# Issuing the branch projections' 512-column matmuls as two of 256 columns into halves of one bank

## The chip, the cores and the metric

The kernel runs on one core of a Trainium2 chip. The metric is the device time of one execution in microseconds (us). Of the kernel before, three runs gave 668.11, 668.73 and 669.14 us, so the median is 668.73 us. The profile is one further execution of the same program, whose span from the first to the last instruction is 666.6 us.

## The reference, cut to what matters

The kernel computes one decoder layer with two parallel branches, in float32, for 256 tokens and a model width of 2048. An attention branch and a gated-MLP branch each give a 256x1024 matrix; each is gated by a SiLU and multiplied by its own projection matrix, and the two results are merged under sigmoid gates:

```python
y_a = (att * jax.nn.silu(z_a)) @ w_proj_a          # (256, 1024) @ (1024, 2048)
y_b = (sgu * jax.nn.silu(z_b)) @ w_proj_b          # (256, 1024) @ (1024, 2048)
merged = jax.nn.sigmoid(g_a) * y_a + jax.nn.sigmoid(g_b) * y_b
return x + merged @ w_out
```

The change touches the two products with `w_proj_a` and `w_proj_b` alone; the big input projection `h @ w_in` and the output product with `w_out` stay as they are.

## The kernel before, in words

**The number format.** Every float32 weight tile and every activation is split into a high part, rounded to the format float32r, and a low part, the remainder (`wh` and `wl`; `zah`, `zal`, `zbh`, `zbl`). ACT makes the high part with a copy and DVE the low part with a subtraction (lines 125 and 126). A product is then three float32r matmuls, low x high, high x high and high x low, into the same accumulator. That is the helper `three` (line 302), whose single `nc.tensor.matmul` at line 307 issues nearly all matmuls of the kernel, so that the profile shows them all under L307 and the tile names tell them apart.

**The stages.** `schedule()` lists 120 weight tiles of 128x2048 in the order in which they are used: the projections q, k, v, za, vb, ub and zb, then four rounds, c = 0 to 3, of a gate projection ("g", eight tiles) and a branch projection ("proj", four tiles), and at the end the output product ("out", sixteen tiles). Most "quad" tiles go through a Strassen-like scheme (`seven`, accumulators named `seven_...` and `acc_...`) or the plain scheme (`direct`).

**The branch projections.** In round c, the tiles q = 0 and 1 belong to `w_proj_a` and q = 2 and 3 to `w_proj_b`; each gives 512 output columns of four 128-row blocks of the contraction. `mm_rows` (line 542) walks over the four blocks `kk` and the two halves `m` of the tokens and calls `three` for each: 4 x 2 x 3 = 24 matmuls a tile, 96 a round, 384 in all. A matmul has a stationary 128x128 piece of `zah`, `zal`, `zbh` or `zbl` (loaded into the array by the matmul itself; the profile shows the load as an own row, LDWEIGHTS on PEld), and 512 moving columns of `wh` or `wl`. It accumulates into a PSUM bank of 512 float32, the tile `y`; a round has four of them, in four of the eight banks.

**Around them.** `turn_z` transposes the gated branch outputs on TensorE (`ps_zb`, line 412) and splits them into high and low parts (lines 506 and 507); for the second branch it runs in the first round's projection, through two banks in turn. After a round's last projection tile `merge` (line 532) multiplies the four banks by the gates and adds them, on DVE. `turn_m` (`ps_mT`) transposes the merged result for the output product.

**What sets the order.** The program is written in the order of the tiles, with side work hung on at given tiles by `at(...)`. Loads of weight tiles are issued on SP three tiles ahead, splits on ACT and DVE two tiles ahead. From the ninth tile on, the order within each engine's queue is decided by the tile framework's scheduler; each engine then works through its own queue in that order, and semaphores hold an instruction back until its inputs and its buffer are ready.

Of the kernel before, what the change touches and what calls it, by code (L numbers as in the profile page):

```python
# [29 lines left out]
B = 512  # L30
# [37 lines left out]
def hybrid_layer_kernel(  # L68
# [9 lines left out]
    nc = tc.nc  # L78
# [24 lines left out]
    raw, wh, wl, th, tl = {}, {}, {}, {}, {}  # L103
# [198 lines left out]
    def three(acc, hi, lo, bh, bl, start, stop, first=False):  # L302
        order = ((lo, bh), (hi, bh), (hi, bl))
        if first:
            order = ((hi, bh), (lo, bh), (hi, bl))
        for n, (a, b) in enumerate(order):
            nc.tensor.matmul(acc, a, b, start=(start and n == 0), stop=(stop and n == 2))  # L307

    BLK = {"12": 0, "11": 1, "22": 2, "21": 3}

    def direct(L, hs, ls, i, kp, start, stop):
# [5 lines left out]
        for c, kh in order:  # L317
            r, col = c // 2, c % 2
            hi = hs[t][:, a + kh, r * P:(r + 1) * P]
            lo = ls[t][:, a + kh, r * P:(r + 1) * P]  # L320
            o = BLK[f"{kh + 1}{col + 1}"] * B
            three(L[c], hi, lo, wh[i][:, o:o + B], wl[i][:, o:o + B], start[c == 3] and kh == 0, stop and kh == 1,
                  first=(i == 0))

    def seven(E, L, i, kp, first, last, started, hs, ls, Fh, Fl):
# [11 lines left out]
        def W(b):  # L337
            o = (BLK[b] - 1) * B
            return wh[i][:, o:o + B], wl[i][:, o:o + B]
# [202 lines left out]
    def mm_rows(acc, hl, i, kts, k0, first, last, by_row=False):  # L542

        order = [(kk, m) for kk in range(4) for m in range(2)]
        if by_row:
            order = [(kk, m) for m in range(2) for kk in range(4)]
        for kk, m in order:
            hi, lo = hl(k0 + kk, m)
            three(acc[m], hi, lo, wh[i][:, kk * B:(kk + 1) * B], wl[i][:, kk * B:(kk + 1) * B],
                  first and kk == 0, last and kk == 3)  # L550

    xres = {}

# [17 lines left out]
    first = {}  # L571
# [91 lines left out]
    for i, (kind, name, c, kp, n) in enumerate(G):  # L663
# [8 lines left out]
        if kind == "quad":  # L672
# [10 lines left out]
            if strassen(i):  # L683
                last = 4 if name == "g" else SK[-1]
# [20 lines left out]
        elif kind == "proj":  # L705
            if n % 2 == 0:
                Y = (Y if n else []) + [bank(E[n + m], f"y{n}_{c}{m}") for m in range(2)]
            z = ("za", "zb")[n // 2]

            def hl(k, m):  # L710
                return (X[z + "h"][:, k, m * P:(m + 1) * P], X[z + "l"][:, k, m * P:(m + 1) * P])

            mm_rows(Y[n // 2 * 2:], hl, i, None, 4 * (n % 2), n % 2 == 0, n % 2 == 1)
            if n == 3:
                merge(c, Y)
        for fn, a in later.pop(i, []):
            a = list(a)
# [66 lines left out]
```

## Time and profile before

| | us |
|---|---|
| median of three runs | 668.73 |
| span of the profiled execution | 666.6 |
| PE busy (matmuls) | 653.9 |
| PEld busy (weight loads) | 539.5 |
| DVE busy | 613.9 |
| ACT busy | 427.1 |

The profile has a page and views that are asked for. On the page, the busy time of an engine is the union of its instructions. The chain of waits goes back from the last instruction, at each step to whatever released it; its pieces have a start, a length, and what they were. A group row gives line, engine, operation, out<-in, the shapes and the count, then the busy time and the mean duration of one. Matmuls are pipelined and their ends are modelled: a matmul row of 512 columns lasts 389 ns though the next one starts 227 ns after it, so that the pace of a stretch is read from starts or from chain pieces (length over count), not from durations.

### The profile page before, as it was taken

To read this page: it belongs to the slowest core of one execution; us is meant where nothing else is said; L and a number is where in the kernel's file an instruction comes from. 1 tells how busy PE (TensorE), PEld (TensorE's weight loads), DVE (VectorE), ACT (ScalarE), POOL (GpSimd) and SP (SyncE) were. 2 spreads that over 40 slices of the span, in tenths; PEclk is the share of its full clock that TensorE was granted. 3 is DMA by queue.
4 is the path that set the end of the run, shared out by engine and by line. 5 is a ranking of instruction groups with operands and counts; after the bars stand their busy time and mean duration, and the time that the engine had idled before them with its cause. 6 is when DMAs were issued, how large, how long until landed. Compare 5 with 4: busy or idle time off the path is not lost.

```text
span 666.6 us, 7860 instructions
## 1 busy us (share of the span) xinstructions
PE 653.9 (98%) x2982; PEld 539.5 (81%) x2982; DVE 613.9 (92%) x606; ACT 427.1 (64%) x563; POOL 30.6 (5%) x28
## 2 busy tenths in 40 slices
PE   8799999999999999999999999999999999999997
PEld 4678888888888888888888788888888888888886
DVE  4589999999999699999999999979989989998996
ACT  7778968856895579774656835555564556746460
POOL 1000501300001004000000000000000000000000
PEclk9989999999999999999999999999999999999999
DMA  8962574555455624744546544935583574747641
GB/s 312 418 228 89 220 255 173 198 196 190 166 182 190 252 69 184 276 165 183 197 145 277 210 132 184 329 116 189 190 331 115 191 270 162 252 148 290 200 183 63
DMA packets 22213, 135.32 MB, mean 203 GB/s; under 512 B 2464, under 2 KB 3104, under 8 KB 7072
## 3 DMA queue, kind: packets, MB, share of 16 engines
q1 hardware_dynamic: 21024, 132.73, 54.1%
q10 hardware_dynamic: 1152, 2.10, 1.0%
q8 instruction: 23, 0.38, 0.2%
q14 instruction: 14, 0.11, 0.0%
HBM read 132.72 MB, written 2.10 MB: 202 GB/s over the span
## 4 chain that ended last, share of the span: by engine, by line
PE 75%; DVE 13%; DMA 5%; issue 4%; ACT 2%; SPq 0%; POOL 0%; DVEq 0%; ACTq 0%
PE acc_g L307 12%; PE y L307 11%; PE acc_out L307 9%; PE seven_g L307 6%; PE acc_v L307 4%; PE acc_k L307 4%; PE acc_za L307 4%; PE acc_ub L307 4%; PE acc_q L307 4%; PE seven_out L307 3%; DMA raw<-in_w 3%; DVE tl L157 3%; PE acc_vb L307 3%; DVE wl L126 2%; DMA xnat<-in_x 2%
## 5 line engine op out<-in xcount | busy, mean ns | idle before, releaser
L154 ACT CAST th<-t 128x1024 fp32r<-128x1024 f32 x104 | 109.3, 1054 | 114.1 <-DVE t L143 57.3
L126 DVE TENSOR_TENSOR wl<-raw,wh 128x2048 fp32r<-128x2048 f32 (+2 forms) x76 | 156.1, 2061 | 21.9 <-ACT wh L125 21.7
L125 ACT CAST wh<-raw 128x2048 fp32r<-128x2048 f32 (+2 forms) x76 | 130.8, 1729 | 47.9 <-PE acc_g L307 18.4
L157 DVE TENSOR_TENSOR tl<-t,th 128x1024 fp32r<-128x1024 f32 x104 | 126.2, 1217 | 3.3 <-ACT th L154 3.3
L155 DVE TENSOR_TENSOR wlp<-raw,whp 128x1536 fp32r<-128x1536 f32 x52 | 91.0, 1750 | 7.1 <-ACT whp L152 7.1
L152 ACT CAST whp<-raw 128x1536 fp32r<-128x1536 f32 x52 | 76.8, 1480 | 29.8 <-DMA raw<-in_w 15.1
L143 DVE TENSOR_TENSOR t<-raw 128x1024 f32<-128x1024 f32 x52 | 63.2, 1216 | 0.2
L307 PE MATMUL acc_g<-wl,xh 128*128 128x512 f32 x96 | 37.4, 389 | 0.0
L307 PE MATMUL acc_g<-wh,xh 128*128 128x512 f32 x96 | 37.4, 389 | 0.0
L307 PE MATMUL acc_g<-wh,xl 128*128 128x512 f32 x96 | 37.3, 389 | 0.0
L146 DVE TENSOR_TENSOR t<-t,raw 128x512 f32<-128x512 f32 x52 | 35.8, 689 | 0.3
L145 DVE TENSOR_TENSOR t<-t,raw 128x512 f32<-128x512 f32 x52 | 35.8, 689 | 0.2
L243 POOL TENSOR_TENSOR rs<-ms,mhalf 128x4 f32<-128x4 f32 x12 | 22.4, 1884 | 122.0 <-DVE ms L242 122.0
L307 PE MATMUL acc_q<-wh,xuh 128*128 128x512 f32 x64 | 25.9, 405 | 0.9 <-ACT wh L125 0.9
L307 PE MATMUL acc_q<-wl,xuh 128*128 128x512 f32 x64 | 26.0, 407 | 0.4 <-DVE wl L126 0.4
L307 PE MATMUL y<-wh,zbl 128*128 128x512 f32 x64 | 25.2, 394 | 0.8 <-DVE zbl L507 0.8
L307 PE MATMUL acc_q<-wh,xul 128*128 128x512 f32 x64 | 25.7, 401 | 0.0
L307 PE MATMUL y<-wh,zal 128*128 128x512 f32 x64 | 25.1, 392 | 0.0
L307 PE MATMUL y<-wl,zah 128*128 128x512 f32 x64 | 25.0, 391 | 0.0
L307 PE MATMUL y<-wl,zbh 128*128 128x512 f32 x64 | 24.9, 390 | 0.0
L307 PE MATMUL y<-wh,zbh 128*128 128x512 f32 x64 | 24.9, 390 | 0.0
L307 PE MATMUL acc_out<-wh,mh 128*128 128x512 f32 x64 | 24.9, 389 | 0.0
(502 smaller groups left out, 1598.4 us busy)
## 6 DMA issues: line engine op xcount, KB each, us to landing
raw<-in_w SPq DMA_DIRECT2D x116, 1024.0 KB, 4.8
raw<-in_w SPq DMA_DIRECT2D x7, 512.0 KB, 8.7
xnat<-in_x SPq DMA_DIRECT2D x2, 1024.0 KB, 13.5
xres<-in_x ACTq DMA_DIRECT2D x8, 256.0 KB, 4.7
out<-out_c SPq DMA_DIRECT2D x5, 256.0 KB, 2.5
xt<-in_xT SPq DMA_DIRECT2D x2, 512.0 KB, 8.5
xt<-in_xT SPq DMA_DIRECT2D x3, 256.0 KB, 9.0
raw<-in_w SPq DMA_DIRECT2D x2, 256.0 KB, 4.2
```

Source lines behind the costliest of these rows:

```text
L125: nc.scalar.copy(h, r)
L126: nc.vector.tensor_tensor(l, r, f(h), op=ALU.subtract)
L143: nc.vector.tensor_tensor(two, r[:, B:3 * B].rearrange("p (a n) -> p a n", a=2), r[:, None, 0:B].to_broadcast([P, 2, B]), op=ALU.add)
L145: nc.vector.tensor_tensor(t[:, 2 * B:3 * B], t[:, 0:B], r[:, 2 * B:3 * B], op=ALU.add)
L146: nc.vector.tensor_tensor(t[:, 3 * B:], t[:, 2 * B:3 * B], r[:, 3 * B:], op=ALU.add)
L152: nc.scalar.copy(wh[i], r[:, B:])
L154: nc.scalar.copy(th[i][:, sl], t[:, sl])
L155: nc.vector.tensor_tensor(wl[i], r[:, B:], f(wh[i]), op=ALU.subtract)
L157: nc.vector.tensor_tensor(tl[i][:, sl], t[:, sl], f(th[i][:, sl]), op=ALU.subtract)
L243: nc.gpsimd.tensor_tensor(dst, ms[:, :n], mhalf[:, :n], op=ALU.pow)
L307: nc.tensor.matmul(acc, a, b, start=(start and n == 0), stop=(stop and n == 2))
```

## The change

`mm_rows` calls a new helper, `three_halves`, in place of `three`. It issues the same three products in the same order, each as two matmuls of 256 moving columns, the first into columns 0 to 255 of the bank and the second into columns 256 to 511. Both have the same stationary piece. Only the first of the six matmuls that open a bank carries the start flag; the group check of the framework is switched off for these matmuls.

```diff
+    def three_halves(acc, hi, lo, bh, bl, start, stop):
+        for n, (a, b) in enumerate(((lo, bh), (hi, bh), (hi, bl))):
+            for h in range(2):
+                sl = slice(h * (B // 2), (h + 1) * (B // 2))
+                nc.tensor.matmul(acc[:, sl], a, b[:, sl], start=(start and n == 0 and h == 0),
+                                 stop=(stop and n == 2), skip_group_check=True)
+
...
         for kk, m in order:
             hi, lo = hl(k0 + kk, m)
-            three(acc[m], hi, lo, wh[i][:, kk * B:(kk + 1) * B], wl[i][:, kk * B:(kk + 1) * B],
-                  first and kk == 0, last and kk == 3)
+            three_halves(acc[m], hi, lo, wh[i][:, kk * B:(kk + 1) * B], wl[i][:, kk * B:(kk + 1) * B],
+                         first and kk == 0, last and kk == 3)
```

The 384 matmul instructions become 768. The framework's scheduler also puts some of the work around them in another order. Three places show it. The first is TensorE's queue in the first round's projection, where `turn_z` transposes the second branch (`ps_zb`, four transposes a row) between projection matmuls (`y`). Before:

```order
L307 MATMUL y_00_3007<-wh_2965,zah 128x512
L307 MATMUL y_00_3007<-wl_2966,zah 128x512
L307 MATMUL y_01_3008<-wh_2965,zal 128x512
L307 MATMUL y_01_3008<-wh_2965,zah 128x512
L412 MATMUL ps_zb_3049<-ident,zb_c_2653 128x128 x4
L307 MATMUL y_01_3008<-wl_2966,zah 128x512
L412 MATMUL ps_zb_3056<-ident,zb_c_2652 128x128 x4
L307 MATMUL y_00_3007<-wh_2965,zal 128x512
```

And of the change, at the same place (a row that ends in x2 is the two halves):

```order
L313 MATMUL y_00_3007<-wh_2965,zal 128x256 x2
L313 MATMUL y_00_3007<-wh_2965,zah 128x256 x2
L313 MATMUL y_00_3007<-wl_2966,zah 128x256
L419 MATMUL ps_zb_3073<-ident,zb_c_2653 128x128 x4
L313 MATMUL y_00_3007<-wl_2966,zah 128x256
L313 MATMUL y_01_3008<-wh_2965,zal 128x256
L419 MATMUL ps_zb_3080<-ident,zb_c_2652 128x128 x4
L313 MATMUL y_01_3008<-wh_2965,zal 128x256
L313 MATMUL y_01_3008<-wh_2965,zah 128x256 x2
```

The third group of transposes stands two and a half old matmuls earlier, the fourth still one old matmul behind it, so eight and a half old matmuls (as halves) are now left behind the fourth where there were six.

The second place is DVE's queue near the end of the gate projection of round 2. `tl` is the low part of the last Strassen tile of that projection, `wl` the low part of a plain tile that is needed later. Before:

```order
L155 TENSOR_TENSOR wlp_3760<-raw_3713,whp_3759 128x1536
L126 TENSOR_TENSOR wl_3793<-raw_3753,wh_3792 128x2048
L157 TENSOR_TENSOR tl_3762<-t_3755,th_3761 128x1024
L126 TENSOR_TENSOR wl_3820<-raw_3790,wh_3819 128x2048
L354 TENSOR_TENSOR g_h<-seven_g_1_3652,g_c_3844 128x512
```

And of the change, for the same tiles under other buffer numbers:

```order
L155 TENSOR_TENSOR wlp_3952<-raw_3905,whp_3951 128x1536
L157 TENSOR_TENSOR tl_3954<-t_3947,th_3953 128x1024
L126 TENSOR_TENSOR wl_3985<-raw_3945,wh_3984 128x2048
L126 TENSOR_TENSOR wl_4012<-raw_3982,wh_4011 128x2048
L361 TENSOR_TENSOR g_h<-seven_g_1_3844,g_c_4036 128x512
```

The second half of `tl` is now ahead of both plain tiles, one 128x2048 subtraction earlier.

The third place is TensorE's queue at the start of the output product, just behind the last projection matmul. `seven_out` and `acc_out` are its accumulators. Before:

```order
L307 MATMUL seven_out_0_4538<-wlp_4423,mh_4383 128x512
L307 MATMUL acc_out_2_4537<-th_4424,ml_4384 128x512
L307 MATMUL acc_out_2_4537<-th_4424,mh_4383 128x512
L307 MATMUL acc_out_0_4535<-whp_4422,ml_4384 128x512
L307 MATMUL acc_out_0_4535<-whp_4422,mh_4383 128x512
```

And of the change:

```order
L307 MATMUL seven_out_0_4922<-wlp_4759,mh_4719 128x512
L307 MATMUL acc_out_0_4919<-whp_4758,ml_4720 128x512
L307 MATMUL acc_out_0_4919<-whp_4758,mh_4719 128x512
L307 MATMUL acc_out_0_4919<-wlp_4759,mh_4719 128x512
L307 MATMUL acc_out_1_4920<-whp_4758,Flm 128x512
```

The two matmuls into `acc_out_2` have moved some nine matmuls back; the group of matmuls at the start of this stage is otherwise the same work.

## The prediction, as it was made before the run

> **What bounds the kernel now.** I read the page's busy shares first, then the chain of waits, then the projection's own rows.
>
> ```profile
> PE 653.9 (98%) x2982; PEld 539.5 (81%) x2982; DVE 613.9 (92%) x606; ACT 427.1 (64%) x563; POOL 30.6 (5%) x28
> ...
> PEclk9989999999999999999999999999999999999999
> ```
>
> TensorE is busy for 98% of the span and DVE for 92%, so the shares alone do not say which of the two decides in the rounds that the change touches. There are as many weight loads as matmuls (2982 each): every matmul brings its own load. The granted clock is at the upper level, 2.4 GHz, all along but for one early slice. The chain, in order of time (start, length, what), settles the first question:
>
> ```profile
> 378.63 0.80 issue
> 379.43 0.69 DVE zbl L507
> 380.17 11.21 PE y L307 x48
> ...
> 431.50 21.76 PE y L307 x96
> ...
> 493.38 21.76 PE y L307 x96
> ...
> 555.26 10.88 PE y L307 x48
> 566.15 1.75 PE ps_mT L412 x16
> 567.89 5.50 PE y L307 x24
> ...
> 574.26 5.46 PE y L307 x24
> ...
> 651.04 11.57 PE acc_out L307 x51
> ```
>
> From 380.17 us to the end of the matmuls every piece is TensorE's own. In the pieces shown stand 48 + 96 + 96 + 48 + 24 + 24 = 336 of the 384 projection matmuls (`y`). Whatever these cost more or less goes straight to the end. The other 48, the first branch of round 0, lie ahead of 379.43, where the chain hangs on DVE. The **pace** of a projection matmul is 21.76 / 96 = 226.7 ns.
>
> ```profile
> 431.34 0.39 PE L307 MATMUL y<-wh,zal 128*128 128x512 f32 x1
> 431.34 0.19 PEld L307 LDWEIGHTS y<-wh,zah 128*128 128x128 f32 x1
> ...
> 431.57 0.39 PE L307 MATMUL y<-wh,zah 128*128 128x512 f32 x1
> 431.57 0.19 PEld L307 LDWEIGHTS y<-wl,zah 128*128 128x128 f32 x1
> ```
>
> These timeline rows show how the two units interleave: the load for the next matmul (`zah`) begins when the present one (`zal`) begins, lasts 0.19 us, and is over some 40 ns before the next matmul starts. So 512 columns hide their load, and the stream of columns sets the pace. With 256 columns the stream is half as long and the load is not.
>
> **What the change does to this.** It removes 384 matmuls of 512 columns and adds 768 of 256, with 768 loads in place of 384. The bytes, the sums and the banks are the same. The question is one number, the pace of a 256-column matmul with its load; 113.3 ns would make no difference. No row of before has this shape, so I bound it. What the load alone allows is shown by the attention scores, 128 columns of plain f32, each record with a load of its own:
>
> ```profile
> 154.40 5.36 PE ps_s L435 x48
> ...
> L435 PEld LDWEIGHTS ps_s<-kT,qT 128*128 128x128 f32 x48 | 5.5, 192 | 0.1
> L307 PEld LDWEIGHTS y<-wh,zah 128*128 128x128 f32 x64 | 12.0, 188 | 2.4
> ```
>
> The scores run at 5.36 / 48 = 111.7 ns a record, though their load rows last 192 ns against the projection's 188: most of a load's row is latency, and one load every 111.7 ns can be had. The transposes (`ps_mT`, 1.75 / 16 = 109.4 ns, quoted above) come to nearly the same.
>
> The **lower bound** is then 111.7 ns: a pair takes 223.3, 3.3 ns less than one matmul before, and 336 x 3.3 = 1.1 us is gained.
>
> For the **upper bound** I ask what in 226.7 ns belongs to the columns and what to the instruction. The early slice at the lower clock helps:
>
> ```profile
> 36.44 0.63 PE L307 MATMUL acc_q<-wh,xuh 128*128 128x512 f32 x1
> ...
> 36.87 0.63 PE L307 MATMUL acc_q<-wl,xuh 128*128 128x512 f32 x1
> ...
> 37.30 0.63 PE L307 MATMUL acc_q<-wh,xul 128*128 128x512 f32 x1
> ```
>
> At 1.2 GHz the same form is issued every 0.43 us, which is 512 columns at one column a cycle (426.7) and nothing else. At 2.4 GHz that would be 213.3; the row says 226.7, so 13.4 ns are extra at the upper level. If all of this were a fixed cost of an instruction, a half would take 106.7 + 13.4 = 120.1 ns, a pair 240.1, and 336 x 13.4 = 4.5 us would be lost. If all of it went with the columns (operand data that cannot be read as fast as the array takes it), a half would take 113.3 and nothing would change. The short records decide where I stand: if a transpose of 128 columns is 256 cycles of array time (106.7 ns), only 109.4 - 106.7 = 2.7 ns of its pace are the instruction's. They also carry four bytes an element, and pay no 13 ns. I **take 2.7 ns fixed**, the rest with the columns: a half is (226.7 - 2.7) / 2 + 2.7 = 114.7 ns, which is above the load's 111.7, so the stream still decides. The sum is 336 x 2.7 = **+0.9 us**; both ends, -1.1 and +4.5, are kept for the range.
>
> The Trainium skill, "TensorE: Matmul & The Clock Gate", section "Back-to-back issue gap", gives the gap of a warm matmul as columns over 2.4 plus 2.5 ns. By it a split costs 2.5 ns, and the sum would be 336 x 2.5 = +0.84 us. By the same rule 512 columns take about 216 ns, which this trace contradicts with 226.7; the rule has no place for the other 11 ns.
>
> **The 48 others** are hidden. In TensorE's timeline (the bracket is idle time and what ended it):
>
> ```profile
> 376.04 0.39 PE L307 MATMUL y<-wh,zah 128*128 128x512 f32 x1
> 376.61 0.66 PE L412 MATMUL ps_zb<-ident,zb_c 128*128 128x128 f32 x4 [0.19 <-DVE zbl L507]
> ...
> 378.94 0.40 PE L307 MATMUL y<-wl,zah 128*128 128x512 f32 x1
> 380.17 0.50 PE L307 MATMUL y<-wh,zbl 128*128 128x512 f32 x1 [0.83 <-DVE zbl L507]
> ```
>
> TensorE twice waits here for DVE's split of the transposed tiles, 0.19 + 0.83 = 1.0 us by the profile. The earlier place of the third transposes moves 2.5 x 0.227 = 0.57 us of projection work from ahead of the first wait to ahead of the second, where 0.83 us of idle time takes it up. At 2.7 ns each the 48 cost 0.13 us, at 13.4 ns 0.64 us, and both fit into the two waits; were that cover gone, this much would be added to the sum. The start of the second branch at 380.17 stays DVE's. I cost this at nothing.
>
> **The other moved work** I cost at nothing too. Where rounds 1 to 3 are concerned the margin is seen in the windows (busy time of PE, PEld, DVE, ACT):
>
> ```profile
> 431.50:453.20 21.70, 21.70 (x98) 17.96 (x97) 16.85 (x15) 12.00 (x10) 0.00 (x0) 1.00 0.43 148
> ...
> 515.10:555.20 40.10, 40.10 (x179) 33.20 (x178) 37.13 (x36) 21.42 (x18) 0.00 (x0) 1.00 0.65 235
> ```
>
> DVE has 4.8 us to spare in the projection of round 1 and 3.0 us in the last gate projection, so subtractions that change places with the merges are caught up again. The thinnest place is the end of the gate projection of round 2:
>
> ```profile
> 484.05 1.21 DVE L157 TENSOR_TENSOR tl<-t,th 128x1024 fp32r<-128x1024 f32 x1
> ...
> 485.51 0.39 PE L307 MATMUL seven_g<-tl,xh 128*128 128x512 f32 x1
> ```
>
> `tl` is ready at 485.26 and used at 485.51, 0.25 us later. The new order puts just this subtraction ahead of a 2.28 us one, so the place gets safer. At the start of the output product the moved pair starts at 580.23 and 580.46:
>
> ```profile
> 580.46 0.39 PE L307 MATMUL acc_out<-th,mh 128*128 128x512 f32 x1
> 580.87 0.50 PE L307 MATMUL acc_out<-whp,ml 128*128 128x512 f32 x1
> ```
>
> Behind it 0.41 us pass where 0.23 would do, and the load gap shows in the longer row: a wait of about 0.3 us that the new order may remove or may repeat elsewhere; I allow 0.4 us on either side.
>
> The profiled execution's 666.6 us become 667.5. The median of the runs lies 2.1 us above that span, and I add the same to both: **669.6 us**.
>
> **The rivals.** *A fixed cost of each instruction* (slower): the 13.4 ns are paid between any two such matmuls, whatever their length. For it: the lower clock would hide such a gap as well as it hides a slow read, and the transposes' slower use of their data may hide it too. Against it: those short records do not show it. +4.5 us, 673.2. It decides against the change from about 4 ns a split on (336 x 4 = 1.3 us).
>
> *A pace as after a pause* (slower): with twice the instructions, and load and stream both near 112 ns, neither can wait for the other without delay. Behind the wait at 380.17 even 512-column matmuls come slower for a while:
>
> ```profile
> 380.51 0.40 PE L307 MATMUL y<-wh,zbh 128*128 128x512 f32 x1
> 380.74 0.39 PE L307 MATMUL y<-wl,zbh 128*128 128x512 f32 x1
> 380.98 0.40 PE L307 MATMUL y<-wh,zbl 128*128 128x512 f32 x1
> ```
>
> Two take 0.47 us, 235 ns each, 8 ns over the pace; at 6 to 8 ns a pair, 336 of them would lose 2.0 to 2.7 us, 670.7 to 671.4. Against it stands that it passes: the piece of 48 from 380.17 on averages 11.21 / 48 = 233.5 ns with the load wait in it, the next ones 226.7.
>
> *The load sets the pace* (no slower, at best a gain): a short stream is read ahead during the load, and a half takes 111.7 ns; -1.1 us, 667.6.
>
> *A load cannot overlap a short matmul* (much slower): each half then waits for its own 188 ns, a pair takes 376, and 336 x 149 ns = 50 us are lost, 718.8. Against it stand the scores, whose loads of 192 ns come every 111.7. The Trainium skill, same page, section "The mechanism", says that LDWEIGHTS overlaps matmuls in flight only where the row group differs; by that rule no load here would be hidden, since all matmuls use the whole array. The trace disagrees: the load at 431.34 runs beside the matmul that starts there.
>
> *The change does not do what it says*: the second load of the same stationary piece could be dropped. Then the stream alone decides, as in my sum.
>
> **How the numbers follow.** My forecast, the stream with a small fixed cost, gets 0.49; the fixed cost 0.25; the pace after a pause 0.12; the load's pace 0.09; no overlap 0.03; the dropped load 0.02, at the forecast's time. A measurement tells about 0.2%, 1.3 us, from no change. Slower by more than that are the fixed cost, the pause's pace, no overlap, and a small tail of the forecast: 0.41. Faster is only the load's pace together with a vanished wait: 0.05. The rest, 0.54, is within. The range goes from the load's pace with a little gain from the order, 667.3, to the fixed cost with a small loss, 673.6; it leaves out no overlap and the tails. The forecast's own range is 668.5 to 670.3.
>
> **What would show it.** The chain piece of a round's projection (192 records) should last 22.0 us (114.7 ns each); 23.1 would be the fixed cost, 21.4 the load's pace, 36 no overlap. Loads should be 3366 in number. TensorE should still be the chain from about 380 us on, and the wait ahead of the second branch in round 0 should be there, shorter. I am wrong if DVE or ACT pieces appear in the chain behind 381 us, or if gate or output matmuls change their pace of 227 ns.

## The result, and the profile after

| | us |
|---|---|
| before, median of four runs | 668.59 (668.11 to 669.14) |
| change, median of four runs | 673.19 (672.65 to 673.33) |
| ratio, with its 95% interval | 1.0063 (1.0048 to 1.0077) |
| span of the profiled execution, before and after | 666.6 and 670.9 |

The change costs 4.6 us by the medians and 4.3 us by the two spans. That lies inside the predicted range, but it is the time of a rival (673.2 us, a fixed cost of each instruction) and not of the forecast (669.6 us, own range 668.5 to 670.3).

On the page of the changed kernel, TensorE's matmuls and loads have the number that was announced, and the granted clock is as before:

```profile
PE 658.6 (98%) x3366; PEld 560.3 (84%) x3366; DVE 615.1 (92%) x606; ACT 427.3 (64%) x563; POOL 30.5 (5%) x28
...
PEclk9989999999999999999999999999999999999999
```

The chain of waits of the changed kernel, in order of time (start, length, what, count), with the pieces that answer to those shown of before:

```profile
380.19 11.78 PE y L313 x96
...
432.12 23.03 PE y L313 x192
...
495.30 23.03 PE y L313 x192
...
558.48 11.52 PE y L313 x96
570.00 1.75 PE ps_mT L419 x16
571.74 5.76 PE y L313 x48
578.38 5.75 PE y L313 x48
...
655.37 11.57 PE acc_out L307 x51
```

From 380.19 us on the chain is TensorE's, as before. A half takes 23.03 / 192 = 120.0 ns, so a pair takes 240 where one matmul took 226.7. Set piece against piece, the projections grew by 0.57 us (round 0, second branch), 1.27 and 1.27 us (rounds 1 and 2) and 0.64 + 0.26 + 0.29 us (round 3), 4.3 us in all. The last piece of the output product starts at 655.37 instead of 651.04 us, 4.33 us later, and is as long as it was. So nearly all of the loss is made in these 672 halves. Between them little changes: the first piece of each gate projection lasts 6.83 instead of 6.80 us, and the stretch from the last projection matmul to the last piece of the output product is 0.1 us shorter.

The timeline of the changed kernel inside round 1 (start, length, engine, operation; rows that end in x2 are two halves in one row):

```profile
432.91 0.40 PE L313 MATMUL y<-wh,zah 128*128 128x256 f32 x2
...
433.03 0.31 PEld L313 LDWEIGHTS y<-wl,zah 128*128 128x128 f32 x2
433.15 0.40 PE L313 MATMUL y<-wl,zah 128*128 128x256 f32 x2
```

A new product begins every 0.24 us, and its loads begin 0.12 us ahead of it, beside the matmul before. Loads still overlap matmuls. Yet a half takes 13.3 ns more than its 256 columns at 2.4 GHz (106.7 ns), which is what a whole matmul took over its 512 (226.7 - 213.3 = 13.4).

The first 48 projection matmuls of round 0 stayed hidden: the second branch starts at 380.19 us where it started at 380.17. Of the two waits for DVE ahead of it (0.19 and 0.83 us) one is left, in the list of waits of the changed kernel (total us, count, longest):

```profile
PE y L313 <- DVE zbl L514: 0.2, 1, 0.2
```

### The profile page after: what moved, and what is told of

It reads as the page before. It is cut to its first block, busy times and chain, and to the rows that moved or that the text cites. A ratio compares the mean times of both kernels' runs of the same rounds, so it can differ in the third digit from the quotient of the medians.

```text
span 670.9 us, 8633 instructions
## 1 busy us (share of the span) xinstructions
PE 658.6 (98%) x3366; PEld 560.3 (84%) x3366; DVE 615.1 (92%) x606; ACT 427.3 (64%) x563; POOL 30.5 (5%) x28
## 4 chain that ended last, share of the span: by engine, by line
PE 63%; DVE 19%; DMA 6%; issue 6%; ACT 5%; POOL 0%; SPq 0%; DVEq 0%; ACTq 0%
PE y L313 12%; PE acc_g L307 12%; PE acc_out L307 9%; PE seven_g L307 6%; PE acc_k L307 4%; DVE tl L157 4%; DMA raw<-in_w 4%; PE acc_ub L307 4%; PE acc_q L307 3%; PE seven_out L307 3%; DVE wl L126 3%; PE acc_vb L307 3%; DVE wlp L155 2%; DVE t L143 2%; DMA xnat<-in_x 2%
## 5 line engine op out<-in xcount | busy, mean ns | idle before, releaser
L313 PE MATMUL y<-wh,zbl 128*128 128x256 f32 x128 | 26.1, 285 | 0.2 <-DVE zbl L514 0.2
L313 PE MATMUL y<-wh,zal 128*128 128x256 f32 x128 | 26.1, 284 | 0.0
L313 PE MATMUL y<-wl,zah 128*128 128x256 f32 x128 | 26.0, 284 | 0.0
L313 PE MATMUL y<-wh,zah 128*128 128x256 f32 x128 | 25.8, 283 | 0.0
L313 PE MATMUL y<-wh,zbh 128*128 128x256 f32 x128 | 25.8, 283 | 0.0
L313 PE MATMUL y<-wl,zbh 128*128 128x256 f32 x128 | 25.8, 283 | 0.0
```

The lines of the kernel that those rows point to most:

```text
L313: nc.tensor.matmul(acc[:, sl], a, b[:, sl], start=(start and n == 0 and h == 0), stop=(stop and n == 2), skip_group_check=True)
```

## The experiments

All of them edit the changed kernel. Where no interval is given, the time is that of one run, beside the kernel before on the same chip. The theory was by then that each matmul instruction pays some 13 ns whatever its length; the rivals were that a change of the bank's half costs this, that the instruction cannot be issued faster than every 120 ns, and that the weight load sets 120 ns. The lines quoted below are pieces of the chain of waits unless another view is named.

**The two halves in another order.** All three products go into the first half of the bank, then all three into the second, so that the written half changes once in three matmuls.

```diff
-        for n, (a, b) in enumerate(((lo, bh), (hi, bh), (hi, bl))):
-            for h in range(2):
+        for h in range(2):
+            for n, (a, b) in enumerate(((lo, bh), (hi, bh), (hi, bl))):
```

> The six matmuls of a product go half by half: three into columns 0 to 255, then three into columns 256 to 511, in place of the two halves in turn. Fixed gap of each instruction: the pace stays at 120.0 ns and the time at 673. If the cost came from changing between the halves of a bank with each matmul: four of six changes are gone, the mean pace falls from 120.0 to about 115.5 ns and the time to about 670. If adding into the same 256 columns twice in a row were slow: the pace rises above 120.

It took 673.16 us (before: 669.17).

```profile
432.53 23.03 PE y L313 x192
```

The piece is the same to 0.01 us. Changing from one half of a bank to the other is not what costs.

**Four matmuls of 128 columns.**

```diff
-            for h in range(2):
-                sl = slice(h * (B // 2), (h + 1) * (B // 2))
+            for h in range(4):
+                sl = slice(h * P, (h + 1) * P)
```

> Each projection matmul is split into four of 128 columns. Fixed gap, with the load as the floor: the stream would allow 53.3 + 13.3 = 66.7 ns, the load 111.7, so 111.7 ns a record, 447 ns for four, 336 x 220 ns = 74 us over the kernel before, 742. Issue limit of 120 ns an instruction: 480 ns for four, 336 x 253 ns = 85 us, 754. If a short matmul hid no load at all, 190 ns or more a record: 848 or more.

It took 790.38 us (before: 669.17).

```profile
389.69 58.13 PE y L313 x273
...
490.06 42.83 PE y L313 x384
```

In round 1 a quarter takes 42.83 / 384 = 111.5 ns. So these float32r instructions can follow each other faster than every 120 ns, and the issue rate does not set the halves' pace. Columns and a fixed 13.3 ns would give 66.6 ns; here the load is the limit, at the pace of the scores in the kernel before (111.7 ns). The load is thus 8.5 ns short of deciding for the halves. The time is 121 us above that of the kernel before, where 111.5 ns for the 336 matmuls on the chain make 74 us, mainly because round 0 ran at the lower clock. The windows (window, length, then busy time of PE, PEld, DVE, ACT and POOL, granted clock, DMA share, GB/s):

```profile
360.00:390.00 30.00, 22.27 (x160) 20.86 (x159) 24.01 (x23) 16.11 (x16) 0.00 (x0) 0.90 0.56 215
390.00:410.00 20.00, 20.00 (x96) 20.00 (x96) 5.40 (x7) 2.22 (x2) 0.00 (x0) 0.50 0.15 53
...
430.00:450.00 20.00, 20.00 (x90) 19.52 (x90) 3.53 (x6) 1.99 (x2) 0.00 (x0) 0.50 0.14 53
450.00:490.00 40.00, 40.00 (x175) 33.00 (x173) 33.51 (x30) 19.52 (x16) 0.00 (x0) 0.97 0.52 184
```

In the chain this is the piece from 389.69 us, 58.13 / 273 = 213 ns a quarter. Against 111.5 ns that is 28 us lost in one round. Most of the rest is a wait ahead of it, from the list of waits,

```profile
PE ps_zb L419 <- DVE zbl L514: 7.7, 1, 7.7
```

and the 48 matmuls of round 0's first branch, which as quarters are too long for the waits that hid them: 48 x (4 x 111.5 - 226.7) ns are 10.5 us.

**Uneven parts, 384 and 128 columns.**

```diff
-            for h in range(2):
-                sl = slice(h * (B // 2), (h + 1) * (B // 2))
+            for sl in (slice(0, 384), slice(384, B)):
...
```

> Each projection matmul is split into 384 and 128 columns in place of 256 and 256. Fixed gap (every float32r matmul takes its columns at 2.4 GHz plus 13.3 ns, whatever its length): the piece of 384 runs at 160.0 + 13.3 = 173.3 ns; the piece of 128 would stream in 66.7 ns and waits for its successor's load, so 111.7 ns as the attention scores; a pair 285 ns, 336 x 58 ns = 19.6 us over the kernel before, 688. Cost that goes with the columns (0.443 ns each): 170.0 ns for the piece of 384, and 281.7 a pair, 687. An instruction every 120 ns at best (issue limit): the piece of 128 takes 120 ns, not 112, and the pair 290 ns, 690.

It took 699.24 us (before: 669.17).

```profile
441.43 27.46 PE y L312 x192
```

The pair takes 27.46 / 96 = 286.0 ns, near the 285 of the fixed price with the load's floor: 384 columns with 13.3 ns extra are 173.3 ns, and the 112.7 ns that remain for the short one are near the quarters' 111.5. Only the sum is measured: in the trace of round 1 a matmul of 384 columns starts 57 to 59 ns behind the one of 128, which starts 227 to 229 ns behind the one of 384, so that this run does not show the price of either part by itself. The time does not answer to that price, since 336 x (286.0 - 226.7) is 19.9 us, and 30.1 were lost. In the list of waits two stand that neither the kernel before nor the change has:

```profile
PE seven_out L307 <- DVE g_c L544: 2.9, 1, 2.9
...
PE ps_zb L418 <- DVE zbl L513: 2.4, 1, 2.4
```

With other sizes the scheduler puts the rows in another order, and TensorE waits for DVE. The two waits are 5.3 of the 10 us. Behind the wait at the transposes the granted clock is lower as well:

```profile
380.00:400.00 20.00, 19.34 (x126) 19.32 (x127) 16.53 (x18) 6.37 (x7) 0.00 (x0) 0.91 0.45 155
```

As an estimate, this costs (1 - 0.91) x 20 = 1.8 us, and the 48 matmuls of round 0's first branch cost another 1.8: they add 48 x 59.3 ns = 2.8 us where the waits that hid them were 1.0 us. About 1 us stays open.

**Half of the stationary columns.** If the load of 128 columns cost the extra time, 64 should cost less.

```diff
+            M = P if start and n == 0 else P // 2
...
-                nc.tensor.matmul(acc[:, sl], a, b[:, sl], start=(start and n == 0 and h == 0),
+                nc.tensor.matmul(acc[:M, sl], a[:, :M], b[:, sl], start=(start and n == 0 and h == 0),
```

> All projection matmuls of 256 columns but the first product of a bank use 64 of the 128 stationary columns, so that the weight load is half as large; half of the output rows get the first product alone. Fixed gap of each instruction: the pace of the narrow records stays at 120.0 ns, time 673. Collision of the weight load with the stream (13.3 ns for a load of 128 columns): about 106.7 + 6.7 = 113.3 ns, time about 669.

It took 669.09 us (before: 669.17).

```profile
431.02 21.83 PE y L314 x192
```

A half takes 113.7 ns, 7 ns over its columns: half of the extra time is gone with half of the stationary columns. This spoke for the load as a part of the price, so three more kernels varied it.

**Whole matmuls with 64 stationary columns, halves with 32, and halves with 64 of the 128 rows.** The edits of the three, in this order:

```diff
+            M = P if start and n == 0 else P // 2
+            nc.tensor.matmul(acc[:M], a[:, :M], b, start=(start and n == 0),
+                             stop=(stop and n == 2), skip_group_check=True)
```

```diff
+            M = P if start and n == 0 else P // 4
...
+                nc.tensor.matmul(acc[:M, sl], a[:, :M], b[:, sl], start=(start and n == 0 and h == 0),
```

```diff
+                nc.tensor.matmul(acc[:, sl], a[:P // 2], b[:P // 2, sl], start=(start and n == 0 and h == 0),
```

> The projection matmuls have all 512 columns again, as before the change, but all except the first product of a bank use 64 of the 128 stationary columns; half of the output rows get the first product alone. The cost belongs to the load (columns at 2.4 GHz plus 13.3 ns for a load of 128 stationary columns, 6.7 for 64): 213.3 + 6.7 = 220.0 ns in place of 226.7, a round's 96 in 21.1 us, 336 x 6.4 ns = 2.1 us under the kernel before. The cost belongs to the columns (0.443 ns each, and the 120 ns of a half come from a load that takes nearly all of the stream's time): 226.7 ns and no change to the kernel before.

> As the run with narrow weights and 256 columns, but 32 stationary columns in place of 64; three quarters of the output rows get the first product alone. The cost belongs to the load: 106.7 + 3.3 = 110.0 ns a record, a round's 192 in 21.2 us, about 1.2 us under the kernel before. The cost belongs to the columns: 113.3 ns as with 64, 21.8 us, the time of the kernel before.

> The halves of 256 columns use 64 of the 128 rows of both operands (half of the contraction is left out); the load has 128 columns of 64 rows. If what counts is the number of stationary columns: 120.0 ns a record, time as with the change, 673. If what counts is the amount of data in the load or the stream: about 113.3 ns, time as before, 669.

They took 669.92, 671.2 and 676.18 us (before: 668.36). One piece of each, in this order:

```profile
432.25 22.07 PE y L312 x96
```

```profile
432.31 22.26 PE y L314 x192
```

```profile
433.99 23.21 PE y L313 x192
```

512 columns with the narrower load take 229.9 ns, more than with the full one (226.7); a quarter of the stationary columns takes 115.9 ns, more than the half of them (113.7); and half of the rows, half of the data in either operand, takes 120.9 ns, no less than all of them. (Its time is 3 us above the 673 that was expected for this pace; why was not followed.) A price of the load fits the second line as little as a price of the data fits the third. With narrower loads the starts are also uneven (223 to 237 ns apart in the first kernel), so that a chain piece is a mean over several spacings. No simple rule held: this is left open below.

**The projections in bfloat16.** High and low parts of the projections' operands are bfloat16 here; rounds 0 and 1 have whole matmuls, rounds 2 and 3 halves.

```diff
+                if G[i][0] == "proj":
+                    wh[i], wl[i] = (x.bitcast(BF16)[:, 0:WORDS] for x in (wh[i], wl[i]))
...
-            three_halves(acc[m], hi, lo, wh[i][:, kk * B:(kk + 1) * B], wl[i][:, kk * B:(kk + 1) * B],
+            (three if G[i][2] < 2 else three_halves)(acc[m], hi, lo, wh[i][:, kk * B:(kk + 1) * B], wl[i][:, kk * B:(kk + 1) * B],
```

> The operands of the branch projections are bfloat16 in place of float32r (so the product is less exact); rounds 0 and 1 use matmuls of 512 columns, rounds 2 and 3 of 256. Any matmul pays 13.3 ns: 226.7 and 120.0 ns. The cost is that of a four-byte load or stream: about 213.3 + 3 = 216 ns and 106.7 + 3 = 109 ns, as the transposes have it, so a round takes 20.8 to 20.9 us whether split or not, and the time falls by 336 x 10 ns = 3 us or more under the kernel before.

It took 670.0 us (before: 668.36). First the timeline of round 1, then a chain piece of round 2:

```profile
435.72 0.38 PE L309 MATMUL y<-wh,zal 128*128 128x512 bf16 x1
...
437.01 0.38 PE L309 MATMUL y<-wh,zal 128*128 128x512 bf16 x1
```

```profile
492.86 20.98 PE y L315 x192
```

Six whole matmuls from 435.72 to 437.01 are 215 ns each, and a half takes 20.98 / 192 = 109.3 ns, 2.6 ns over its columns. The extra time shrinks from 13 ns to under 3 with the format, at the same 128 stationary and 256 moving columns. The load changes with the format too, as the group rows of the halves' loads show, here in bfloat16 and then of the change in float32r:

```profile
L315 PEld LDWEIGHTS <-zah 128*128 128x128 bf16 x128 | 12.5, 98 | 1.5
```

```profile
L313 PEld LDWEIGHTS y<-wh,zah 128*128 128x128 f32 x128 | 19.9, 192 | 0.0
```

A load's row lasts 98 ns instead of 192, so this run alone does not tell whether the load or the stream of columns makes the difference. The Trainium skill, "TensorE: Matmul & The Clock Gate", section "Back-to-back issue gap", gives 2.5 ns over the columns; the bfloat16 rows agree with it (2.6), the float32r rows do not (13.3).

The shorter projections did not make the kernel faster. In the list of waits and in the chain of this kernel, at the start of the output product:

```profile
PE acc_out L309 <- DVE ml L516: 1.9, 1, 1.9
```

```profile
577.30 2.20 DVE Flm L301
579.50 0.61 DVE ml L516
580.12 0.04 issue
580.16 2.25 PE acc_out L309 x6
```

TensorE comes to the output product earlier and waits there for DVE's split of the merged result. Before, this piece of the chain was TensorE's own. Behind the wait the granted clock is lower for a while, 0.89 in the mean of 15 us where the kernel before has 1.00:

```profile
575.00:590.00 15.00, 13.13 (x67) 10.56 (x66) 14.21 (x15) 7.94 (x8) 0.00 (x0) 0.89 0.41 157
```

The last projection matmul starts 2.0 us earlier than before (577.33 instead of 579.33 us). The wait takes 1.9 of that back, and the lower clock, (1 - 0.89) x 15 = 1.7 us as an estimate, is about the 1.6 us by which the time is above that of the kernel before.

**Plain float32.** The halves' operands are taken as float32 instead of float32r; the trace then shows two records for each matmul.

```diff
-                nc.tensor.matmul(acc[:, sl], a, b[:, sl], start=(start and n == 0 and h == 0),
+                nc.tensor.matmul(acc[:, sl], f(a), f(b[:, sl]), start=(start and n == 0 and h == 0),
```

> The halves of 256 columns are computed in plain float32, the same bytes, which the profile shows as two records for each matmul, each with a load, and whose array time for a column is two cycles in place of one: 213.3 ns a record. If the 13.3 ns are the price of a load of 128 four-byte columns, a record takes 226.7 ns, a round's 384 take 87.0 us, time 336 x (4 x 226.7 - 226.7) ns = 228.5 us over the kernel before, 897. If the 13.3 ns arise only where four-byte columns stream at one a cycle, a record takes 216 to 218 ns, a round 83 to 84 us, time about 882 to 885.

It took 912.86 us (before: 668.59).

```profile
492.62 82.88 PE y L313 x384
```

A record of 256 columns takes 82.88 / 384 = 215.8 ns. With two cycles for a column that is 213.3 + 2.5 ns. Its load is of 128 columns of four bytes, like the float32r one, and its rows last 190 ns, and yet the extra is 2.5 ns: neither the load nor the width of the data makes the 13 ns by itself. That the load has more time here is no reason either, since a whole float32r matmul leaves it as much (226.7 ns) and pays 13.4. In these runs the 13 ns appear only where float32r columns stream at one a cycle. The time is above the expected one because at this length the 48 matmuls of round 0's first branch are no longer hidden: 384 x (4 x 215.8 - 226.7) ns = 244 us, and 668.6 + 244 is 913.

**272 and 240 columns.** The parts are uneven by 16, to see whether the extra time follows a raster of columns.

```diff
-            for h in range(2):
-                sl = slice(h * (B // 2), (h + 1) * (B // 2))
+            for sl in (slice(0, 272), slice(272, B)):
...
```

> Each projection matmul is split into 272 and 240 columns. Fixed gap of each float32r matmul with a full load: 113.3 + 13.3 = 126.7 and 100.0 + 13.3 = 113.3 ns, a pair 240.0 ns as with two halves, a round's 192 in 23.0 us, time 673. Starts that fall on a raster of 13.3 ns (which also gives 226.7 = 17 steps for 512 and 120.0 = 9 for 256): 120.0 for the 272 columns and the load's 111.7 for the 240, 231.7 a pair, 22.2 us, 670. Cost that goes with the columns: 120.4 and 111.7, the same 232.

It took 690.44 us (before: 668.59).

```profile
441.27 22.67 PE y L312 x192
```

A pair takes 236.1 ns, 11.4 ns extra for each part in the mean instead of 13.3. The starts are uneven here: the next matmul starts 122 to 130 ns behind a part of 272 columns and 106 to 112 ns behind one of 240. The projections' pace accounts for 336 x 9.4 ns = 3.2 us of the 21.9 lost. The rest comes from the order. The list of waits has

```profile
PE ps_zb L418 <- DVE zbl L513: 8.0, 1, 8.0
...
PE acc_out L307 <- DVE ml L513: 4.2, 1, 4.2
```

and DVE's timeline shows the first of them, here in this kernel and then in the change:

```profile
378.09 1.76 DVE L155 TENSOR_TENSOR wlp<-raw,whp 128x1536 fp32r<-128x1536 f32 x1 [1.79 <-ACT whp L152]
379.89 2.29 DVE L126 TENSOR_TENSOR wl<-raw,wh 128x2048 fp32r<-128x2048 f32 x1
382.10 1.28 DVE L513 TENSOR_TENSOR zbl<-ps_zb,zbh 128x512 fp32r<-128x512 f32 x2
```

```profile
375.90 1.28 DVE L514 TENSOR_TENSOR zbl<-ps_zb,zbh 128x512 fp32r<-128x512 f32 x2
377.25 2.29 DVE L126 TENSOR_TENSOR wl<-raw,wh 128x2048 fp32r<-128x2048 f32 x1
379.46 1.28 DVE L514 TENSOR_TENSOR zbl<-ps_zb,zbh 128x512 fp32r<-128x512 f32 x2
```

The first pair of `zbl`, which frees the two transpose banks, stands behind two splits of weight tiles (`wlp`, which starts after 1.79 us of idle time, and `wl`) and starts at 382.10 us; in the change it starts at 375.90 us, ahead of `wl`. TensorE's next row, the third group of transposes, needs a bank and holds up all that is queued behind it. Behind both waits the granted clock is lower as well:

```profile
380.00:400.00 20.00, 17.16 (x130) 17.17 (x131) 17.31 (x17) 7.38 (x8) 0.00 (x0) 0.83 0.28 97
...
590.00:600.00 10.00, 5.78 (x31) 4.90 (x30) 8.32 (x9) 6.23 (x6) 0.00 (x0) 0.75 0.11 46
...
600.00:610.00 10.00, 9.10 (x35) 6.78 (x34) 8.97 (x9) 3.95 (x4) 0.00 (x0) 0.74 0.39 140
```

The last two windows lie about the second wait, of 4.2 us. The pace, the two waits and the lower clock, at most 3.4 + 5.1 us by these windows, cover the whole loss.

**The price in another place.** The projections are whole again, and the 360 float32r matmuls of the output product are issued in halves.

```diff
+            if G[i][1] == "out":
+                three_halves(L[c], hi, lo, wh[i][:, o:o + B], wl[i][:, o:o + B], start[c == 3] and kh == 0, stop and kh == 1)
+                continue
...
-            three(acc, hi, lo, bh, bl, first if any(acc is e for e in E) else not started, last and any(acc is e for e in E))
+            (three_halves if G[i][1] == "out" else three)(acc, hi, lo, bh, bl, first if any(acc is e for e in E) else not started, last and any(acc is e for e in E))
...
-            three_halves(acc[m], hi, lo, wh[i][:, kk * B:(kk + 1) * B], wl[i][:, kk * B:(kk + 1) * B],
+            three(acc[m], hi, lo, wh[i][:, kk * B:(kk + 1) * B], wl[i][:, kk * B:(kk + 1) * B],
```

> The projections have 512 columns again as before the change; the 360 matmuls of the output product, all of them on the chain of waits, are split into halves in their place. Fixed gap: 360 x 13.3 ns = 4.8 us over the kernel before, less up to 0.4 us that waits at the start of this stage take up: 672.9 to 673.5. If the price belonged to the projections' place or tiles: no such number, less than 1 us.

The median is 673.34 us (671.79 to 674.02, ten runs) against 668.59 of thirteen runs before, a ratio of 1.0062 (1.0043 to 1.008).

```profile
431.34 21.76 PE y L307 x96
...
611.58 19.44 PE acc_out L313 x162
```

The projections are back at 226.7 ns, and the output product has 19.44 / 162 = 120.0 ns a half. 360 x 13.3 ns are 4.8 us; 4.75 were measured. The price belongs to the instruction, not to the projections, their banks or their neighbours.

## Why the prediction was right in places and failed in one

**Right: where the cost falls.** TensorE bounds the rounds, 336 of the 384 splits lie on the chain, the other 48 vanish in round 0's waits for DVE, and the loads overlap. Taking 13.3 ns for a split, 336 of them are 4.5 us; the pieces show 4.3. The difference is mostly where the matmuls before the change were already slower than 226.7 ns: the 48 of round 0 (233.5 ns in the mean) and the last 48 of round 3 (229.2 and 227.5).

**Right: the signs announced for each rival.** The round's piece was to be 23.1 us for the fixed cost and is 23.03; there are 3366 loads, so none is dropped; 36 us for no overlap and 21.4 us for the load's pace are both out. The pace as after a pause would have been 2.0 to 2.7 us, also out. The load's floor that the lower bound took from the scores is real, 111.5 ns in the quarters, but the halves do not come down to it.

**Wrong: "I take 2.7 ns fixed, the rest with the columns."** This is the step that failed, by a factor of five. The working before it was sound: the rows at the lower clock give 13.4 ns extra at the upper one, and the two ends, all with the instruction or all with the columns, were named. I then chose between them by the short records, with the words that they "also carry four bytes an element, and pay no 13 ns". They do carry four bytes, but they stream a column every two cycles. The plain float32 run shows that a record of 256 columns in that format pays the same 2.5 ns as the transposes' 2.7, while float32r records of the same 256 columns pay 13.3. The nearest rows in length were not rows of the same kind. Besides, the transposes' 109.4 ns had been named in the prediction itself as nearly the pace of the load, so that they could say little of what an instruction costs. Since no row of the kernel before had float32r at another length, it could not tell; the forecast should have stayed with the two ends and given the upper one more than a quarter of the chance. That the time lies in the range is owed to this upper end, to which the forecast gave 0.25, and not to the forecast's own term: 336 x 2.7 ns = 0.9 us were forecast and 4.3 to 4.6 us measured.

The sum by the Trainium skill's section "Back-to-back issue gap" (page "TensorE: Matmul & The Clock Gate"), 0.84 us, fell with it for this format.

**Right here, but not by its reason: the moved work costs nothing.** In the change the pieces between the projections are within 0.03 us of their old lengths, and of the 0.4 us allowed at the output product 0.1 are seen. But I had argued from DVE's spare time. The runs with 384 + 128 and 272 + 240 columns have nearly the same work on DVE (618.3 and 617.9 us busy; the change 615.1), and their orders cost several us in single waits (8.0 and 4.2 us in the second). What saved the change, as far as the traces show, is that its order kept both pairs of `zbl` where they were in DVE's queue (they start within 0.03 us of their old times); no run varied the order alone.

**Settled and open.** Shown: in float32r, with 128 stationary columns, a matmul of 256 or 512 columns takes 13.3 ns over its columns, in two stages of the kernel, and splitting pays it again. Shown not to be the cause: the bank's half, the rate of issue, the amount of data in the rows, four-byte loads by themselves. Open: what inside TensorE takes the 13.3 ns, and why it becomes 7.0 ns (64 stationary columns, 256 moving), 16.6 ns (64, 512), 9.2 ns (32, 256) or 11.4 ns (parts of 272 and 240). Neither a price of the load, nor a constant gap, nor a raster of columns fits all of these. That a float32r load disturbs a stream of one float32r column a cycle while both run remains untested: every case that pays 13 ns has both, and no run changes one of the two formats without the other. None of these kernels was faster than the one before.

## What to carry to other kernels

Take the price of one more instruction from rows of the same format and the same columns per cycle. A row of equal length in another format can be off by a factor of five, and where there is none, keep both ends with like chances. Count it only for the instructions on the chain, and compare the queues' order after any change in the number or size of instructions, since the new order that came with other sizes cost up to 8 us in one wait here. A shorter TensorE stage is worth only what the next wait for DVE leaves of it, and behind such a wait the granted clock can be lower for some us, which must be counted with it.

## What the runs showed of the hardware that was not expected

- The extra time of a matmul depends on the format: 13.3 ns in float32r, 2.6 ns in bfloat16, 2.5 ns for a record in plain float32, each with 256 moving and 128 stationary columns (the bfloat16 load is also shorter, 98 ns a row).
- Fewer stationary columns shorten a float32r half irregularly: 120.0 ns with 128, 113.7 with 64, 115.9 with 32; a whole matmul even got longer, from 226.7 to 229.9 ns.
- After 7.7 us without a matmul in round 0 (30.00 - 22.27 in the first of its windows above), the granted clock of the kernel with quarters was 0.50 from 390 to 450 us, though TensorE was busy in all of that time; it came back in the gate matmuls of 512 columns that followed. After a wait of 8.0 us at the same place, the kernel with parts of 272 and 240 columns had 0.83 from 380 to 400 us and 1.00 from 400 to 420 us. Shorter waits were followed by a lower clock too: 0.91 over 20 us with a wait of 2.4 us (384 + 128 columns), 0.89 over 15 us with one of 1.9 us (bfloat16).
